# Conditioning vectors moved off the tensor engine: scale 2 and shift 2 to VectorE, three quarters of gate 1 to GpSimd

## The chip, the cores and the metric

The kernel runs on one core of one Trainium2 chip. The engines are TensorE (PE; PEld is its weight load), VectorE (DVE), ScalarE (ACT), GpSimd (POOL) and SyncE (SP), which in the kernel before issues all loads. The metric is the device time of one execution in microseconds. The times are medians of runs; the profile is of one execution.

## The reference

One layer of a hybrid decoder on x of 256 tokens by 2048. A conditioning vector c gives six vectors of 2048: shift, scale and gate for the mixers (`sh1`, `sc1`, `g1`) and for the channel mixer (`sh2`, `sc2`, `g2`).

```python
mod = (cond @ w_mod[l] + b_mod[l]).reshape(B, 6, D)      # cond = silu(c)
sh1, sc1, g1, sh2, sc2, g2 = [mod[:, i, None, :] for i in range(6)]
h = rmsnorm(x, norm_mix[l]) * (1.0 + sc1) + sh1
proj = f32(h @ w_in[l])
...                                                      # GLA, gated DeltaNet, pooling, forgetting attention
y = jnp.concatenate([y_a, y_b, y_c, y_d], axis=-1) @ w_out[l]
x = x + g1 * y
h = rmsnorm(x, norm_ffn[l]) * (1.0 + sc2) + sh2
x = x + g2 * conv_ffn(h, ...)
```

`w_mod` is 2048 by 12288, 8 MB for each 1024 of its columns. All is float32.

## The kernel before

The work goes in stages. First, shift 1 and scale 1 are summed on DVE in four groups of 512, and the input projection follows group by group (`gdn`, `extras`). From about 240 us on come the four mixers, with what is left of the input projection between them (`ex`), in the order `ORDER = "gpfd"`; then the output projection in five chunks of columns (`project`; the first into `ext`, the others into `wot`), and from about 543 us the channel mixer, whose matmuls write `fpt`. Large matmuls take each weight in two halves: `load_split` loads `wr`, ACT rounds it to `wh`, DVE subtracts to get `wl`.

The vectors wanted later are computed in the background of the mixers. A job is 1024 columns of scale 2 (`s0`, `s1`), shift 2 (`h0`, `h1`) or gate 1 (`g0`, `g1`), 16 blocks of 128 rows each. `gemv` does one job: it loads a block `wm` (128x1024, 512 KB) and multiplies it by `cond`. It has two ways:

- on PE: `cond` is broadcast to 32 columns as the weight, and four matmuls of 128x512 write four strips of 32 rows in one PSUM tile `bgt`; ACT copies the tile to `wr`, and matmuls with `sel` add the strips;
- on DVE: `accumulate` adds `wm * cond` to the tile `ga`, one instruction for each block. A matmul with `ones` then adds the 128 rows.

`to_col` puts the result along the partitions (scale, shift), `to_row` copies it to all rows (gate 1, read by the output projection as `g1t`). Which job goes where is said by two lists, and `paced` lets each list go on by its rate with every step of `ex`. A scheduler then orders all instructions, engine by engine; each engine and each queue runs its own in that order.

```python
ON_PE, PE_RATE = "s0 s1 h0", 0.38
ON_DVE, DVE_RATE = "h1 g0 g1", 0.69
```

POOL has the small powers (`rqk`, `ls`, `oss`: reciprocal square roots for the mixers), fills of zeros, and twelve compares `mk` near the start.

Of the kernel before, what the change touches and what calls it, by code (L numbers as in the profile page):

```python
# [8 lines left out]
F32 = mybir.dt.float32  # L9
# [40 lines left out]

ORDER = "gpfd"

ON_PE, PE_RATE = "s0 s1 h0", 0.38
ON_DVE, DVE_RATE = "h1 g0 g1", 0.69


def _consts():
# [16 lines left out]
def trunk_kernel(ctx: ExitStack, tc: tile.TileContext, x, c, w_mod, b_mod, norm_mix, norm_ffn, w_in,  # L74
# [18 lines left out]
    def kt_(shape, name, dt=F32):  # L93
        return keep.tile(shape, dt, name=name, tag=name)

    def mm(o, l, r, start=True, stop=True):
        PE.matmul(o, lhsT=l, rhs=r, start=start, stop=stop, skip_group_check=True)  # L97

    def tt(o, a, b, op):
        V.tensor_tensor(out=o, in0=a, in1=b, op=op)  # L100
# [28 lines left out]
    sel = kt_([P, 2], "sel")  # L129
    V.memset(sel, 0.0)  # L130
    for o in (0, 32, 64, 96):
        V.memset(sel[o:o + 1, o // 32 % 2:o // 32 % 2 + 1], 1.0)

    V1 = kt_([P, P], "V1")
    V2 = kt_([P, 54], "V2")
# [27 lines left out]
        return wh, wl  # L163


    last_wm = [None]

    def accumulate(ga, src, k, first=True):
        if k == 0 and first:
            tsc(ga, src, cond[:, k:k + 1], None, ALU.mult)  # L170
        else:
            stt(ga, src, cond[:, k:k + 1], ga, ALU.mult, ALU.add)

    def gemv(col0, done, pst=None, ready=lambda: True, bias=None):


        acc = pst() if pst else keep.tile([P, 1024], F32, name="ga", tag="ga")
        if bias is not None:
            G.memset(acc, 0.0)
            nc.sync.dma_start(acc[0:1], bias)  # L180
        for k in range(0, KT, 2):
            wms = []
            for kk in range(2):
                wms.append(wp.tile([P, 1024], F32, name="wm", tag="wm", bufs=4))
                last_wm[0] = nc.sync.dma_start(wms[kk], wm_v[:, k + kk, col0:col0 + 1024])
            for kk in range(2):
                wm = wms[kk]
                if not pst:
                    accumulate(acc, wm, k + kk, bias is None)
                    continue  # L190
                for c in range(2):
                    o = 64 * kk + 32 * c
                    mm(acc[o:o + 32], cond[:, k + kk:k + kk + 1].to_broadcast([P, 32]), wm[:, c * 512:c * 512 + 512],
                       start=k == 0, stop=k == KT - 2)
            if k == KT - 2:
                while not ready():
                    yield
                with tc.high_priority():
                    if pst:
                        gr = wp.tile([P, 1024], F32, name="wr", tag="wr", bufs=5)[:, 0:512]  # L200
                        S_.copy(gr, acc)
                        done([(gr, sel[:, c:c + 1]) for c in range(2)])
                    else:
                        done([(acc[:, c * 512:c * 512 + 512], ones) for c in range(2)])
# [23 lines left out]
    with ExitStack() as ph:  # L228
# [59 lines left out]
        with ExitStack() as st:  # L288
# [184 lines left out]
                    yield from pair(p, done[p], g + 1)  # L473
                    done[p] = g + 1

            def jobs(seq, pst):
                col = pst or (ext)
                for job in seq.split():
                    kind, n = job[0], int(job[1])
                    k0, col0 = 8 * n, dict(s=4, h=3, g=2)[kind] * D + n * 1024  # L480
                    if kind == "s":
                        yield from gemv(col0, to_col(s2, 4, k0, nffn, col), pst)
                    elif kind == "h":
                        yield from gemv(col0, to_col(sh2, 3, k0, None, col), pst)
                    else:
                        yield from gemv(col0, g1_row(n, bgt), None,
                                        lambda: "gf"[n] in emitted and "s" in emitted, b_mod[:, col0:col0 + 1024])

            emitted = set()

            def marked(steps):
                yield from steps
                emitted.add("s")


            g1t = [None, None]

            def g1_row(n, row):
                def f(parts):
                    name = ("gv", "fv")[n]  # L500
                    g1t[n] = cp.tile([P, 1024], F32, name=name, tag=name)
                    to_row(g1t[n], 0, row)(parts)
# [41 lines left out]


        bgp = ph.enter_context(tc.tile_pool(name="bgp", bufs=1, space=PSUM))
        mx = ph.enter_context(ExitStack())
        gdp = mx.enter_context(tc.tile_pool(name="gdp", bufs=2, space=PSUM, reuse_waits="tile"))
        oxp = mx.enter_context(tc.tile_pool(name="oxp", bufs=3, space=PSUM, reuse_waits="tile"))
# [190 lines left out]
        def gla(lp):  # L740
# [66 lines left out]
            for cc in range(NC - 1):  # L807
                t, os_ = cc // 2, slice((cc % 2) * CH, (cc % 2) * CH + CH)
                b = oxt().rearrange("p (f n) -> p f n", n=256)
                for f in range(2):  # L810
                    mm(b[:, f], kE2[os_, t, f * P:f * P + P], v[os_, t, f * 256:f * 256 + 256])
                s = lt([P, 2, 256], "Sg", bufs=3)
                G.memset(s, 0.0)
# [10 lines left out]
            onl = [lt(W4, f"onl{t}", tag="E", bufs=2) for t in range(NT)]  # L824
            for t in range(NT):
                b = oxt()
                for h in range(4):
                    mm(b[:, h * P:h * P + P], at[h % 2][:, t, h // 2], v[:, t, h * P:h * P + P], start=h == 0)
                for cc in (2 * t, 2 * t + 1):
                    if cc == 0:  # L830
                        continue
                    os_ = slice((cc % 2) * CH, (cc % 2) * CH + CH)
                    for f in range(2):
                        mm(b[os_, f * 256:f * 256 + 256], qT[:, f, cc * CH:cc * CH + CH], Sg[cc][:, f], start=False)
                for h in range(4):
                    jk = lt([P, P], "jl", tag="qE")
                    act(jk, b[:, h * P:h * P + P], AF.Square, accum_out=ls[:, t, h:h + 1])
                tsc(ls[:, t], ls[:, t], 1.0 / P, EPS, ALU.mult, ALU.add)
                G.tensor_tensor(out=ls[:, t], in0=ls[:, t], in1=mhalf[:, 0:4], op=ALU.pow)
                for h in range(4):  # L840
                    act(onl[t][:, h], b[:, h * P:h * P + P], AF.Copy, scale=ls[:, t, h:h + 1])
            act(flat(pr[:, 4:8]), flat(pr[:, 4:8]), AF.Silu)
# [60 lines left out]

        ex = extras(NG - 1)

        rate, owed = (PE_RATE, DVE_RATE), [0.0, 0.0]

        def paced(steps):
            for _ in steps:
# [220 lines left out]
```

## Time and profile before

| | us |
|---|---|
| median of 3 runs | 1309.63 |
| lowest and highest | 1309.63, 1311.2 |
| the profiled execution | 1305.91 |
| its span, first to last instruction | 1304.1 |

In the profile's rows a line such as L97 can be that of a helper (`mm` is L97, `tt` L100, `stt` L103), so tiles tell more than lines. A row of instructions has the engine, the operation, out<-in, the count, and times; with three numbers and slashes they are the shortest, the median and the longest in ns. A row of a stretch has its bounds, its length, then for each engine the busy time and the number of instructions.

### The profile page before, as it was taken

How to read it: one execution, taken by the hardware profiler on the slowest of the kernel's cores; microseconds unless marked ns; L12 is line 12 of the kernel's file. 1: busy time of each engine (PE TensorE's matmuls, PEld its weight loads, DVE VectorE, ACT ScalarE, POOL GpSimd, SP SyncE). 2: the span in 40 equal slices, each digit the busy share in tenths (PEclk: the TensorE clock that was granted, in tenths of full speed). 3: DMA queues.
4: the chain of work that ended last, by engine and by line, in shares of the span. 5: the costliest groups of instructions: out<-in, count | busy, mean ns of one | idle time of the engine just before them, and what ended most of it. 6: DMA issues, size and time to landing. Idle time of an engine off the chain costs nothing.

```text
span 1304.1 us, 20373 instructions
## 1 busy us (share of the span) xinstructions
PE 1251.1 (96%) x7927; PEld 1094.0 (84%) x7927; DVE 893.8 (69%) x1201; ACT 638.1 (49%) x1000; POOL 23.5 (2%) x31
## 2 busy tenths in 40 slices
PE   2799999999999999999999999999999999999996
PEld 1799999898876788888888888888888888888896
DVE  7679797989763397676656565765666597974543
ACT  3455344774354444565545554555555454443432
POOL 0200000010000100000000000000000000000000
PEclk8799999999999999999999999999999999999998
DMA  8999998796567997466666666666666699875652
GB/s 324 287 367 376 321 335 295 257 335 216 163 236 242 325 331 262 146 183 189 186 187 191 182 176 197 191 184 188 190 184 181 193 372 366 316 249 193 193 180 81
DMA packets 174231, 311.94 MB, mean 239 GB/s; under 512 B 16172, under 2 KB 65331, under 8 KB 173495
## 3 DMA queue, kind: packets, MB, share of 16 engines
q1 hardware_dynamic: 174135, 310.65, 73.3%
q8 instruction: 62, 1.02, 0.3%
q14 instruction: 34, 0.28, 0.1%
HBM read 308.51 MB, written 2.10 MB: 238 GB/s over the span
## 4 chain that ended last, share of the span: by engine, by line
PE 92%; DMA 5%; DVE 1%; ACT 1%; issue 1%; SPq 1%; POOLq 0%; ACTq 0%; DVEq 0%
PE fpt L97 57%; PE ext L97 16%; PE wot L97 5%; PE acc L97 4%; PE gdt L97 4%; DMA wm<-in_w_mod_dram 4%; PE bgt L97 3%; PE oxt L97 2%; DVE ga L103 1%; DMA wr<-in_w_in_dram 1%; DMA wsm<-in_w_in_dram 0%; ACT xT L1011 0%; DVE wl L100 0%; ACT wh L115 0%; PE oxt L873 0%
## 5 line engine op out<-in xcount | busy, mean ns | idle before, releaser
L100 DVE TENSOR_TENSOR wl<-wr,wh 128x1024 fp32r<-128x1024 f32 x384 | 468.4, 1223 | 294.2 <-ACT wh L115 293.2
L115 ACT CAST wh<-wr 128x1024 fp32r<-128x1024 f32 x384 | 402.5, 1051 | 491.4 <-PE fpt L97 306.6
L97 PE MATMUL fpt<-bigA,wh 128*128 128x512 f32 x1408 | 485.7, 397 | 2.1 <-DVE bigA L103 2.1
L97 PE MATMUL fpt<-bigA,wl 128*128 128x256 f32 x1408 | 376.2, 281 | 0.0
L97 PEld LDWEIGHTS fpt<-bigA,wh 128*128 128x128 f32 x1408 | 261.1, 188 | 62.5 <-issue 2.2
L97 PEld LDWEIGHTS fpt<-bigA,wl 128*128 128x128 f32 x1408 | 259.7, 188 | 4.8
L103 DVE SCALAR_TENSOR_TENSOR ga<-wm,cond,ga 128x1024 f32<-128x1024 f32 x139 | 177.8, 1279 | 11.3 <-DMA wm<-in_w_mod_dram 10.3
L97 PE MATMUL fpt<-wl,AH 128*128 128x512 f32 (+1 forms) x440 | 152.9, 348 | 0.0
L97 PE MATMUL fpt<-wh,AL 128*128 128x512 f32 (+1 forms) x440 | 152.5, 347 | 0.0
L97 PE MATMUL fpt<-wh,AH 128*128 128x512 f32 (+1 forms) x440 | 142.6, 348 | 0.0
L97 PE MATMUL ext<-bigA,wh 128*128 128x256 f32 x768 | 137.1, 280 | 0.0
L97 PEld LDWEIGHTS ext<-bigA,wh 128*128 128x128 f32 x768 | 117.3, 189 | 3.1 <-DVE dS L100 0.8
L97 PE MATMUL ext<-bigA,wl 128*128 128x256 f32 x384 | 107.4, 280 | 1.7 <-DVE wl L100 1.7
L97 PEld LDWEIGHTS fpt<-wh,AH 128*128 128x128 f32 x440 | 83.3, 189 | 10.8 <-ACT wh L115 0.2
L97 PEld LDWEIGHTS fpt<-wh,AL 128*128 128x128 f32 x440 | 83.3, 189 | 10.6 <-issue 0.2
L97 PEld LDWEIGHTS fpt<-wl,AH 128*128 128x128 f32 x440 | 83.3, 189 | 10.5 <-issue 0.2
L97 PEld LDWEIGHTS ext<-bigA,wl 128*128 128x128 f32 x384 | 72.1, 188 | 3.0 <-DVE wl L100 1.9
L97 PE MATMUL acc<-bigA,wh 128*128 128x256 f32 x384 | 69.0, 286 | 3.5 <-ACT bigA L115 2.8
L97 PE MATMUL ext<-wh,bigA 128*128 128x256 f32 (+1 forms) x320 | 69.5, 309 | 0.0
L97 PE MATMUL wot<-wh,bigA 128*128 128x512 f32 (+1 forms) x256 | 63.0, 337 | 0.0
L97 PEld LDWEIGHTS acc<-bigA,wh 128*128 128x128 f32 x384 | 59.6, 195 | 3.9 <-ACT bigA L115 2.9
L97 PEld LDWEIGHTS ext<-wh,bigA 128*128 128x128 f32 x320 | 53.0, 193 | 5.5 <-ACT wh L115 1.7
(340 smaller groups left out, 1187.4 us busy)
## 6 DMA issues: line engine op xcount, KB each, us to landing
wm<-in_w_mod_dram SPq DMA_DIRECT2D x192, 512.0 KB, 6.3
wr<-in_w_in_dram SPq DMA_DIRECT2D x88, 512.0 KB, 9.1
wr<-in_ffn_w_gate_dram SPq DMA_DIRECT2D x88, 512.0 KB, 4.0
wr<-in_ffn_w_up_dram SPq DMA_DIRECT2D x88, 512.0 KB, 3.9
wr<-in_ffn_w_down_dram SPq DMA_DIRECT2D x88, 512.0 KB, 4.4
wr<-in_w_out_dram SPq DMA_DIRECT2D x32, 512.0 KB, 4.4
xt<-in_x_dram SPq DMA_DIRECT2D x2, 1024.0 KB, 7.1
bigC<-in_x_dram SPq DMA_DIRECT2D x2, 1024.0 KB, 10.5
```

The source lines that it names most:

```text
L97: PE.matmul(o, lhsT=l, rhs=r, start=start, stop=stop, skip_group_check=True)
L100: V.tensor_tensor(out=o, in0=a, in1=b, op=op)
L103: V.scalar_tensor_tensor(out=o, in0=a, scalar=s, in1=b, op0=op0, op1=op1)
L115: S_.copy(hi, src)
```

## The change

- The way over PE is gone. `s0`, `s1`, `h0` and `h1` are summed on DVE.
- Gate 1 is cut into four jobs of 512 columns. `g0`, `g1`, `g2` are done by a new `gemv_pool` on POOL: for each of 16 blocks POOL issues the load of `pm` (128x512), multiplies it by `cond` in place and adds it to `gp`. There are two `pm` and three `gp`. `g3` is done on DVE, with two blocks of 512 columns in one `wm`.
- `wm` has three buffers instead of four; the GLA states `Sg` share buffers with `dd` and `E`, and `onl` is made later.
- DVE's list goes on during the output projection, with its own rate.

```diff
-ON_PE, PE_RATE = "s0 s1 h0", 0.38
-ON_DVE, DVE_RATE = "h1 g0 g1", 0.69
+ON_POOL, POOL_RATE, LAG = "g0 g1 g2", 2.2, 6
+ON_DVE, DVE_RATE, DVE_RATE_OUT = "s0 s1 h0 g3 h1", 1.4, 0.6
...
-    def gemv(col0, done, pst=None, ready=lambda: True, bias=None):
+    def gemv(col0, done, bias=None, n=1024, ready=lambda: True):
-        acc = pst() if pst else keep.tile([P, 1024], F32, name="ga", tag="ga")
+        acc = keep.tile([P, n], F32, name="ga", tag="ga", padded_shape=[P, 1024])
...
-                wms.append(wp.tile([P, 1024], F32, name="wm", tag="wm", bufs=4))
-                last_wm[0] = nc.sync.dma_start(wms[kk], wm_v[:, k + kk, col0:col0 + 1024])
-            for kk in range(2):
-                wm = wms[kk]
-                if not pst:
-                    accumulate(acc, wm, k + kk, bias is None)
-                    continue
-                for c in range(2):
-                    o = 64 * kk + 32 * c
-                    mm(acc[o:o + 32], cond[:, k + kk:k + kk + 1].to_broadcast([P, 32]), wm[:, c * 512:c * 512 + 512],
-                       start=k == 0, stop=k == KT - 2)
+            for kk in range(0, 2, nk):
+                wm = wp.tile([P, 1024], F32, name="wm", tag="wm", bufs=3).rearrange("p (k n) -> p k n", n=n)
+                last_wm[0] = nc.sync.dma_start(wm, wm_v[:, k + kk:k + kk + nk, col0:col0 + n])
+                wms += [wm[:, i] for i in range(nk)]
+            for kk in range(2):
+                accumulate(acc, wms[kk], k + kk, bias is None)
...
+            def gemv_pool(col0, done, bias, n, ready):
+                acc = bp[0].tile([P, 512], F32, name="gp", tag="gp", bufs=3)
+                G.memset(acc, 0.0)
+                G.dma_start(acc[0:1], bias)
+                for k in range(KT):
+                    pm = bp[0].tile([P, 512], F32, name="pm", tag="pm", bufs=2)
+                    G.dma_start(pm, wm_v[:, k, col0:col0 + 512])
+                    G.tensor_tensor(out=pm, in0=pm, in1=cond[:, k:k + 1].to_broadcast([P, 512]), op=ALU.mult)
+                    G.tensor_tensor(out=acc, in0=acc, in1=pm, op=ALU.add)
+                    yield
+                for _ in range(LAG):
+                    yield
+                while not ready():
+                    yield
+                with tc.issue_after(last_mm[0].ins):
+                    done([(acc, ones)])
...
-            bg = [marked(jobs(ON_PE, bgt)), jobs(ON_DVE, None)]
+            bg = [jobs(ON_POOL), jobs(ON_DVE)]
...
-                s = lt([P, 2, 256], "Sg", bufs=3)
+                s = lt([P, 2, 256], "Sg", tag="dd" if cc < 2 else "E", bufs=2)
...
-            for b_ in bg:
-                for _ in b_:
-                    pass
+            for _ in bg[0]:
+                pass
...
                 wh, wl = load_split(wo_v, ks[0], nk, c0, w)
+                owed[1] += DVE_RATE_OUT
+                while owed[1] >= 1:
+                    owed[1] -= 1
+                    next(bg[1], None)
```

What the scheduler makes of it, at two places. On PE, near the end of the mixers before the change (`gdt` is DeltaNet, `oxt` the attention, `bgt<-wm` a gate, scale or shift block):

```order
L97 MATMUL bgt_4700<-wm_4751,cond_77 32x512 x2
L97 MATMUL gdt_3111<-dS_2740,bigC_2607 64x128 x2
L873 MATMUL oxt_4518<-ident_61,p_4535 128x128 x2
L97 MATMUL bgt_4700<-wm_4757,cond_77 32x512 x2
L97 MATMUL gdt_3117<-bigC_2607,kti_2741 128x128 x4
L97 MATMUL oxt_4545<-pt_4543,fv_94 128x256
L97 MATMUL oxt_4545<-pt_4543,fv_94 128x128
L97 MATMUL oxt_4554<-pr_92 128x128
L97 MATMUL oxt_4554<-ct_85,la_4549 128x128
L97 MATMUL oxt_4554<-ngr_91,idr_90 128x128
L97 MATMUL bgt_4700<-wm_4759,cond_77 32x512 x2
L97 MATMUL gdt_3126<-X_2743,bigC_2607 64x128 x4
```

After the change no such rows are there. In their place stand four row copies of gate 1, the last of them among the first matmuls of the second projection chunk (`wot_5091` and `wot_5092`; `wh_5095` and `wh_5119` are its first two loads):

```order
L97 MATMUL wot_5092<-wh_5119,bigA_4860 128x512
L97 MATMUL wot_5091<-wh_5119,bigA_4860 128x512
L97 MATMUL wot_5091<-wl_5120,bigA_4860 128x512
L97 MATMUL wot_5091<-wh_5119,bigA_4860 128x512
L97 MATMUL wot_5092<-wh_5119,bigA_4860 128x512
L97 MATMUL wot_5092<-wl_5120,bigA_4860 128x512
L97 MATMUL bgt_4857<-gp_4790,ones_65 128x512
L97 MATMUL wot_5092<-wh_5119,bigA_4860 128x512
L97 MATMUL wot_5091<-wh_5137,bigA_4860 128x512
```

The copy waits for `gp_4790`, the third sum on POOL, and all that stands behind it on PE waits with it. In the kernel before, all of PE's blocks were done ahead of the projection, and the last copies were of sums on DVE.

On POOL before the change, from the fills to the mixers' last power:

```order
L813 MEMSET Sg_3984 128x512
L813 MEMSET Sg_3993 128x512
L813 MEMSET Sg_4002 128x512
L577 TENSOR_TENSOR rqk_2688<-rqk_2688,mhalf_78 128x16
L179 MEMSET ga_3719 128x1024
L839 TENSOR_TENSOR ls_4008<-ls_4008,mhalf_78 128x4 x2
L726 TENSOR_TENSOR oss_3132<-oss_3132,mhalf_78 128x4 x2
L179 MEMSET ga_4784 128x1024
```

The queue holds nothing else in this stretch, and its powers and fills follow each other. After the change, around the same power `rqk` (the first two steps' sums, then the loads of the next two):

```order
L468 TENSOR_TENSOR pm_3221<-pm_3221,cond_71 128x512
L468 TENSOR_TENSOR pm_3225<-pm_3225,cond_71 128x512
L469 TENSOR_TENSOR gp_3218<-gp_3218,pm_3221 128x512
L469 TENSOR_TENSOR gp_3218<-gp_3218,pm_3225 128x512
L467 DMA pm_3266<-in_w_mod_dram 128x512
L467 DMA pm_3270<-in_w_mod_dram 128x512
L579 TENSOR_TENSOR rqk_2685<-rqk_2685,mhalf_72 128x16
L468 TENSOR_TENSOR pm_3266<-pm_3266,cond_71 128x512
L468 TENSOR_TENSOR pm_3270<-pm_3270,cond_71 128x512
L469 TENSOR_TENSOR gp_3218<-gp_3218,pm_3266 128x512
```

The power stands behind two steps and ahead of the other 46. From the fifth step on a load, a product and an addition follow each other one by one:

```order
L467 DMA pm_3414<-in_w_mod_dram 128x512
L469 TENSOR_TENSOR gp_3218<-gp_3218,pm_3410 128x512
L467 DMA pm_3454<-in_w_mod_dram 128x512
L468 TENSOR_TENSOR pm_3414<-pm_3414,cond_71 128x512
L469 TENSOR_TENSOR gp_3218<-gp_3218,pm_3414 128x512
L468 TENSOR_TENSOR pm_3454<-pm_3454,cond_71 128x512
L467 DMA pm_3458<-in_w_mod_dram 128x512
L469 TENSOR_TENSOR gp_3218<-gp_3218,pm_3454 128x512
L467 DMA pm_3517<-in_w_mod_dram 128x512
L468 TENSOR_TENSOR pm_3458<-pm_3458,cond_71 128x512
L469 TENSOR_TENSOR gp_3218<-gp_3218,pm_3458 128x512
```

The load of a step is issued behind the addition two steps before it, which frees its buffer. The two powers `oss`, which DeltaNet waits for, stand behind some 40 of the 48 steps.

More of the change, by code (lines that the diff above doesn't have):

```diff
@@ L96, in mm @@
     def mm(o, l, r, start=True, stop=True):
-        PE.matmul(o, lhsT=l, rhs=r, start=start, stop=stop, skip_group_check=True)
+        last_mm[0] = PE.matmul(o, lhsT=l, rhs=r, start=start, stop=stop, skip_group_check=True)
     def tt(o, a, b, op):
@@ L127, in trunk_kernel @@
     V.memset(ones, 1.0)
[L129 to L132, printed above, removed]
     V1 = kt_([P, P], "V1")
@@ L198, in gemv @@
                 with tc.high_priority():
[L199 to L204, printed above, removed]
+                    done([(acc[:, c:c + 512], ones) for c in range(0, n, 512)])
             yield
@@ L478, in jobs @@
+            def jobs(seq):
                 for job in seq.split():
                     kind, n = job[0], int(job[1])
-                    k0, col0 = 8 * n, dict(s=4, h=3, g=2)[kind] * D + n * 1024
+                    k0 = 8 * n
                     if kind == "s":
-                        yield from gemv(col0, to_col(s2, 4, k0, nffn, col), pst)
+                        yield from gemv(4 * D + n * 1024, to_col(s2, 4, k0, nffn, bgt))
                     elif kind == "h":
-                        yield from gemv(col0, to_col(sh2, 3, k0, None, col), pst)
+                        yield from gemv(3 * D + n * 1024, to_col(sh2, 3, k0, None, bgt))
@@ L485, in jobs @@
                     else:
-                        yield from gemv(col0, g1_row(n, bgt), None,
-                                        lambda: "gf"[n] in emitted and "s" in emitted, b_mod[:, col0:col0 + 1024])
+                        c0 = 2 * D + n * 512
+                        how = (gemv_pool if n < 3 else gemv)
+                        yield from how(c0, g1_row(n // 2, n % 2 * 512, bgt), b_mod[:, c0:c0 + 512], n=512,
+                                       ready=lambda: "gf"[n // 2] in emitted)
@@ L489, in trunk_kernel, with g1_row @@
             emitted = set()
-            def marked(steps):
-                yield from steps
-                emitted.add("s")
             g1t = [None, None]
-            def g1_row(n, row):
+            def g1_row(n, c, row):
                 def f(parts):
-                    name = ("gv", "fv")[n]
-                    g1t[n] = cp.tile([P, 1024], F32, name=name, tag=name)
-                    to_row(g1t[n], 0, row)(parts)
+                    if g1t[n] is None:
+                        name = ("gv", "fv")[n]
+                        g1t[n] = cp.tile([P, 1024], F32, name=name, tag=name)
+                    to_row(g1t[n], c, row)(parts)
@@ L546, in trunk_kernel @@
         bgp = ph.enter_context(tc.tile_pool(name="bgp", bufs=1, space=PSUM))
+        bp[0] = ph.enter_context(tc.tile_pool(name="bp", bufs=1, reuse_waits="tile"))
         mx = ph.enter_context(ExitStack())
@@ L823, in gla @@
             ls = lt([P, NT, 4], "ls")
-            onl = [lt(W4, f"onl{t}", tag="E", bufs=2) for t in range(NT)]
+            onl = []
             for t in range(NT):
@@ L839, in gla @@
                 G.tensor_tensor(out=ls[:, t], in0=ls[:, t], in1=mhalf[:, 0:4], op=ALU.pow)
+                onl.append(lt(W4, f"onl{t}", tag="E", bufs=2))
                 for h in range(4):
```

7 lines of the change are left out of this document (3 added, 4 removed).

## Prediction

> **What bounds the kernel now.** I read the page's busy times and its chain first, then the busy times by stretch, then the rows of the tiles that the change moves, and last the rows of the two engines that get the work.
>
> ```profile
> span 1304.1 us, 20373 instructions
> PE 1251.1 (96%) x7927; PEld 1094.0 (84%) x7927; DVE 893.8 (69%) x1201; ACT 638.1 (49%) x1000; POOL 23.5 (2%) x31
> PE 92%; DMA 5%; DVE 1%; ACT 1%; issue 1%; SPq 1%; POOLq 0%; ACTq 0%; DVEq 0%
> 240.00:265.00 25.00, 23.72 (x189) 19.76 (x188) 24.53 (x45) 16.20 (x31) 0.00 (x0) 1.00 0.78 264
> 265.00:442.00 177.00, 176.85 (x1351) 140.92 (x1349) 116.90 (x210) 87.57 (x195) 6.74 (x4) 1.00 0.72 242
> 442.00:541.00 99.00, 99.00 (x547) 84.56 (x547) 72.88 (x83) 49.81 (x88) 4.71 (x4) 1.00 0.82 287
> ```
>
> TensorE (PE) carries 92% of the chain that ended last. The change lies between 240 and 541 us (the mixers and the output projection). In the last three rows the columns behind the length are the busy time of PE, its weight loads, VectorE (DVE), ScalarE and GpSimd (POOL), then granted clock, DMA share and GB/s. PE is full there at clock 1.00; DVE has 60 of 177 us free from 265 to 442, POOL nearly all. So a matmul taken out of this stretch is worth its time, as long as nothing else comes to end last.
>
> **What leaves the tensor engine.**
>
> ```profile
> L97 PE MATMUL bgt<-wm,cond x192: 592/592/617, 245.5 to 437.9; 128*32 128x512 f32 x192
> 240.00:541.00 301.00, 47.65 (x248) 1.00 0.76 259
> 406.60 1.95 PE L97 MATMUL bgt<-sel,wr 128*128 128x1 f32 x16
> 445.00:541.00 96.00, 4.08 (x8) 1.00 0.82 287
> ```
>
> The first row is the work itself. The second is PE's busy time on the tile `bgt` alone: 47.65 us, with four narrow matmuls lying side by side. In it are three additions of the four strips (`bgt<-sel,wr`, third row, 3 x 1.95) and the four row copies of gate 1 (last row, 4.08). So the products take 47.65 - 5.85 - 4.08 = 37.7 us. The additions shrink from 16 records to 8, which saves 3 x 1 us. Sum: 40.6 us off PE. The ends are 0 (if PE then only waits) and 43.6 (47.65 less the row copies); I take 40.6, since PE shows no gap in these stretches. The three ScalarE copies of the strips go too; ScalarE is half idle, so I count nothing.
>
> **What DVE gets.**
>
> ```profile
> 284.00:478.00 194.00, 128.59 (x232) 1.00 0.73 251
> 284.00:478.00 194.00, 30.70 (x24) 1.00 0.73 251
> 284.00:478.00 194.00, 27.01 (x23) 1.00 0.73 251
> L103 DVE SCALAR_TENSOR_TENSOR ga<-wm,cond,ga x139: 1268/1279/1286, 12.7 to 1152.4; 128x1024 f32<-128x1024 f32 x139
> L100 DVE TENSOR_TENSOR pr<-ext,pr 128x512 f32<-128x512 f32 x24 | 16.4, 685 | 7.1 <-PE ext L97 7.0
> ```
>
> The first three rows are DVE alone from 284 to 478 us (why these ends, below): in all, on the gate and scale sums `ga`, and on the weight halves `wl`. By the order after the change, DVE has 39 sums of 1024 columns and 16 of 512 in the same stretch of work: 39 x 1.279 + 16 x 0.685 (nearest row of 512 columns) = 61 us for 30.7. So its work there is 128.6 + 30 = 159 us. That alone is more than the 194 - 40 = 154 us which the shortened stretch would have.
>
> **What POOL gets: the term that decides.** Each of 48 steps is a load of 128x512 that POOL issues, a product and an addition. POOL has no such row, so I bound them.
>
> ```profile
> L813 POOL MEMSET Sg<- 128x512 f32 x3 | 1.5, 527 | 171.8 <-DVE bigA L100 171.8
> L179 POOL MEMSET ga<- 128x1024 f32 x4 | 3.8, 952 | 632.0 <-PE fpt L97 558.9 <-PE bgt L97 61.3 <-PE ext L97 11.8
> L393 POOL TENSOR_SCALAR mk<-ct x12: 523/527/1587, 43.8 to 51.2; 128x128 uint8<-128x128 f32 x12
> L185 SPq DMA_DIRECT2D wm<-in_w_mod_dram x128: 327/340/1432, 188.7 to 1142.8; - x128
> DMA to landing us min/median/max: 3.5/6.3/9.9
> ```
>
> Below, a product costs at least the write of 512 columns, 0.53 us; above, four times the compare of 128 columns, 4 x 0.527 = 2.1 us. It reads two operands of 512, so the nearest row is the one that moves 1024 columns, 0.95 us. With 0.2 us for waiting on the instruction before it I take 1.15. The Trainium skill's "GPSIMD Engine Reference" (Elementwise — side-by-side cycle accounting) gives 4497 ns for an addition of 2048 columns; a quarter of that is an estimate of 1.1 us, so by it the sum would hardly move. Issuing a load costs 0.33 to 1.43 us, the ends of SP's row for the same tensor; no POOL row is nearer, so I take the middle, 0.9. Undisturbed, a step is 2 x 1.15 + 0.9 = 3.2 us.
>
> It will be disturbed:
>
> ```profile
> 43.72 1.28 DVE L103 SCALAR_TENSOR_TENSOR ga<-wm,cond,ga 128x1024 f32<-128x1024 f32 x1
> 43.81 1.59 POOL L393 TENSOR_SCALAR mk<-ct 128x128 uint8<-128x128 f32 x1 [31.19 <-DMA ct<-in_cst_dram]
> 443.66 1.01 POOL L726 TENSOR_TENSOR oss<-oss,mhalf 128x4 f32<-128x4 f32 x1 [71.44 <-DMA wr<-in_w_out_dram]
> 451.72 1.22 DVE L100 TENSOR_TENSOR wl<-wr,wh 128x1024 fp32r<-128x1024 f32 x1
> 451.96 1.85 POOL L726 TENSOR_TENSOR oss<-oss,mhalf 128x4 f32<-128x4 f32 x1 [7.29 <-DVE oss L109]
> 279.80 1.21 DVE L100 TENSOR_TENSOR wl<-wr,wh 128x1024 fp32r<-128x1024 f32 x1
> 280.04 3.77 POOL L577 TENSOR_TENSOR rqk<-rqk,mhalf 128x16 f32<-128x16 f32 x1 [55.09 <-ACT ag L112]
> 281.15 1.28 DVE L103 SCALAR_TENSOR_TENSOR ga<-wm,cond,ga 128x1024 f32<-128x1024 f32 x1
> ```
>
> Twelve equal compares take 0.53 us each, but the first takes 1.59: it began while DVE was in a sum until 45.00. Two equal powers take 1.01 and 1.85: the second began while DVE was in a `wl` until 452.94. Each time the extra, 1.06 and 0.84 us, is what was left of the DVE instruction, less a tenth. So a POOL instruction that reads waits for the end of a DVE instruction with two SBUF inputs, and the sums and `wl` are all such. Of DVE's 159 us, 61 + 27 + some 20 (smaller ones) = 108 are of this kind, about half of the stretch. A product that comes at random then waits 0.5 x 0.6 = 0.3 us; in strict turns it waits a whole 1.2. I take 0.65, in the lower part, since half of DVE's time doesn't block. A step is 3.2 + 2 x 0.65 = 4.5 us; the ends are 3.2 and 5.6.
>
> The last two rows speak against the page that would make it worst. The Trainium skill's "SBUF — State Buffer" (Who interferes with whom) says that the two engines share a read port, and that whichever starts first holds it for its whole instruction. The power from 280.04 ran to 283.81, yet DVE's sum at 281.15 passed in its usual 1.28 us. That fits if POOL lets go once its 16 columns are read. With 512 columns the read is most of the instruction, and no run here shows that case.
>
> **When PE needs it.** The third POOL sum is waited for by a matmul behind 23 of the 24 first matmuls of the second projection chunk.
>
> ```profile
> 473.01 36.17 PE wot L97 x158
> ```
>
> That is 473.0 + 23 x 36.17/158 = 478 us now, hence 284 to 478 above. After the change it is due at 478 - 40.6 + 1 (one row copy more lies ahead) = 438 us. POOL does only two steps before the power `rqk`, which stands ahead of the third in its queue and ends at 283.8. So 46 steps and 6 us of its other work (four small powers of 1.01, four fills) remain: 284 + 6 + 46 x 4.5 = 497 us. PE waits 497 - 438 = 59 us in all; some of it falls earlier, at the first two POOL rows and at the `oss` powers, which also queue on POOL, but that isn't added. A check without waits: DVE's 108 us and 92 products at 1.0 us of reading, one after the other, end at 484.
>
> **The sum.** 59 - 40.6 = +18 us: about 1322 for the span and 1324 for the profiled time. The profiled execution took 1305.91 us, 3.7 less than the median of 1309.63, so against the median it is 1328.
>
> At nothing I count: `wm` with three buffers instead of four (a sum that is late holds its load, and behind that SP's queue of `wr` loads and so `wl`; the cover is PE's own wait; without it each case costs up to the 2.1 us that a sum waits for `wm` at most now); the same in the last stage, where gate 2 is summed beside 96% PE work; `Sg` and `onl` in shared buffers.
>
> ```profile
> DVE ga L103 <- DMA wm<-in_w_mod_dram: 10.3, 13, 2.1
> ```
>
> **Rivals.**
>
> 1. *Faster: POOL is hardly held.* Then a step is 3.2 to 4.0 us. At 3.4 POOL ends at 446, PE waits 8 us, and DVE's 159 us from 284, 95% packed, end at 451: 13 us of wait against 40.6, so -27 and 1282. It decides from 4.1 us a step on ((438 + 40.6 - 290)/46). For it: DVE stands idle for 65 of 194 us now. Against: the two waits of 1.06 and 0.84 us.
> 2. *Strict turns.* Each POOL instruction waits for a whole DVE one: 5.6 us a step, end at 548, +69, 1379. The skill's rule of the held port would give this, because DVE would always have one waiting. Against: the sum at 281.15.
> 3. *The loads end last.* With two buffers a step can't be shorter than half of issue, landing, two products and two waits: (0.9 + 6.3 + 2.3 + 1.3)/2 = 5.4 us, end at 538, +59, 1369. For it: 6.3 us median to landing. Against: these loads are 256 KB, not 512; at 4.2 us landing it gives 4.35 and hides.
> 4. *No change.* A step of 4.05 to 4.15 us.
>
> **How the numbers follow.** Forecast (4.2 to 5.2 us a step, 1314 to 1360): 0.40. Rival 1: 0.34. Rival 2: 0.08. Rival 3: 0.12. Rival 4: 0.06. About 0.2%, 2.6 us, is what a measurement of this kernel can tell from no change. So slower 0.60, same 0.06, faster 0.34. The range runs from just below rival 1's time, 1280, to 1365, which leaves out the upper rivals and the ends of the forecast, about 0.2; the forecast's own range is 1314 to 1360.
>
> **What the next profile shows.** Right: `bgt<-wm,cond` is gone; POOL is about full from 284 us, with products of over 1.15 us where DVE runs a sum or a `wl`, and adjacent products of one sum 4 to 5 us apart; PE idles for tens of us at `bgt<-gp`, waiting for POOL; `fpt` begins near 565 instead of 543 us, and from there on nothing differs. Wrong: products at 0.5 to 1.0 us, or no wait beside DVE (rival 1); PE waiting on `wl` instead of `gp`, which would make DVE the bound; POOL idle before each product until a load (rival 3).

## The result, and the profile after

| | before | after |
|---|---|---|
| median of the runs, us | 1309.63 | 1360.28 |
| lowest and highest, us | 1306.98, 1311.2 | 1358.42, 1364.99 |
| the profiled execution, us | 1305.91 | 1360.08 |

The changed kernel is slower: ratio 1.0398, with a 95% interval from 1.0376 to 1.0419. That is +51 us, where +18 was forecast (1328).

Of the changed kernel's page the span, the busy times, and the engines' shares of the chain that ended last:

```profile
span 1358.3 us, 20138 instructions
PE 1247.2 (92%) x7735; PEld 1108.5 (82%) x7735; DVE 980.6 (72%) x1228; ACT 638.3 (47%) x997; POOL 191.2 (14%) x180
PE 72%; DVE 12%; DMA 7%; issue 4%; ACT 2%; POOL 1%; SPq 1%; POOLq 0%; ACTq 0%; DVEq 0%
```

TensorE's share of the chain fell from 92 to 72%, and VectorE's rose from 1 to 12%. GpSimd, which the prediction made the end, has 1%. The stretches of the mixers and of the output projection in the changed kernel (columns as in the prediction: PE, PEld, DVE, ACT, POOL, then clock, DMA share, GB/s):

```profile
300.00:350.00 50.00, 39.89 (x302) 38.14 (x301) 50.00 (x51) 17.56 (x25) 39.64 (x32) 0.90 0.72 220
350.00:400.00 50.00, 45.19 (x329) 40.24 (x328) 49.71 (x62) 21.11 (x41) 36.08 (x31) 0.93 0.81 259
400.00:450.00 50.00, 35.26 (x193) 28.35 (x193) 47.19 (x55) 18.57 (x52) 44.58 (x44) 0.83 0.56 167
450.00:500.00 50.00, 36.20 (x203) 28.78 (x202) 40.75 (x61) 20.13 (x66) 20.56 (x20) 0.81 0.78 255
500.00:550.00 50.00, 41.39 (x166) 32.49 (x165) 28.10 (x29) 17.93 (x31) 19.38 (x16) 0.81 0.42 136
```

VectorE is full from 300 to 450 us (146.9 of 150). TensorE stands still for a fifth of that time, and its granted clock, 1.00 there in the kernel before, is 0.83 to 0.93, and 0.81 from 450 to 550 us. So TensorE's busy time fell only from 1251.1 to 1247.2 us, although 40 us of its work are gone. The stretch from 240 us to the channel mixer's first large matmul, first row before, second after:

```profile
240.00:548.20 308.20, 304.10 (x2121) 249.40 (x2119) 219.15 (x349) 160.12 (x325) 12.14 (x9) 1.00 0.75 256
```
```profile
240.00:602.40 362.40, 301.09 (x1923) 265.03 (x1923) 304.08 (x393) 159.41 (x321) 181.45 (x161) 0.89 0.68 215
```

TensorE stands still for 61.3 us there instead of 4.1. By the prediction's 40.6 us of removed work 263.5 us of the 304.1 would be left; they took 301.1, which fits the mean clock (263.5/0.89 is 296). So the stretch got 57 us of standing still and 38 us of slower work, less 40.6 us of removed work: the 54 us by which it is longer.

The channel mixer's large matmuls begin later by all of the difference. First row before, second after; the numbers behind the durations are the first and the last start:

```profile
L97 PE MATMUL fpt<-bigA,wh x1408: 388/397/502, 548.2 to 1044.4; 128*128 128x512 f32 x176
```
```profile
L97 PE MATMUL fpt<-bigA,wh x1408: 388/397/475, 602.4 to 1098.5; 128*128 128x512 f32 x176
```

From the first to the last start it is 496.2 us before and 496.1 after: nothing was lost behind the projection.

Why is VectorE full? Its groups in the changed kernel from 280 to 540 us (busy us, mean ns of one, then idle time before them):

```profile
L103 DVE SCALAR_TENSOR_TENSOR ga<-wm,cond,ga 128x1024 f32<-128x1024 f32 x43 | 66.3, 1541 | 4.7 <-DMA wm<-in_w_mod_dram 4.4
L100 DVE TENSOR_TENSOR wl<-wr,wh 128x1024 fp32r<-128x1024 f32 x28 | 40.8, 1456 | 11.3 <-ACT wh L115 11.3
L103 DVE SCALAR_TENSOR_TENSOR ga<-wm,cond,ga 128x512 f32<-128x512 f32 x16 | 19.3, 1205 | 0.1
L100 DVE TENSOR_TENSOR bigA<-pr,bigA 128x256 fp32r<-128x256 f32 x16 | 15.3, 982 | 5.7 <-ACT bigA L115 5.7
L789 DVE COPY_PREDICATED at<-mk,oxt 128x256 f32<-128x256 uint8 x12 | 6.2, 531 | 0.0
L100 DVE TENSOR_TENSOR pr<-ext,pr 128x512 f32<-128x512 f32 x8 | 5.4, 675 | 0.0
```

A sum of 1024 columns takes 1.54 us instead of 1.28, a weight half 1.46 instead of 1.22, a `bigA` half 0.98 instead of 0.42. All of these read two tensors from SBUF. The last two rows, with one operand in PSUM (`oxt`, `ext`), take what they always took. The timeline of the changed kernel near 302 us shows the mechanism (start, duration, engine):

```profile
301.42 1.04 POOL L468 TENSOR_TENSOR pm<-pm,cond 128x512 f32<-128x512 f32 x1 [2.00 <-DMA pm<-in_w_mod_dram]
...
301.62 1.91 DVE L103 SCALAR_TENSOR_TENSOR ga<-wm,cond,ga 128x1024 f32<-128x1024 f32 x1
...
302.53 2.15 POOL L469 TENSOR_TENSOR gp<-gp,pm 128x512 f32<-128x512 f32 x1
...
303.46 2.31 DVE L100 TENSOR_TENSOR wl<-wr,wh 128x1024 fp32r<-128x1024 f32 x1
...
304.64 2.02 POOL L468 TENSOR_TENSOR pm<-pm,cond 128x512 f32<-128x512 f32 x1
```

GpSimd's product runs undisturbed to 302.46. The sum began at 301.62 and ends at 303.53, which is 1.1 us behind the product's end. The addition ends 1.15 us behind the sum, the weight half 1.1 us behind the addition, the next product 0.9 us behind the weight half. They take strict turns, and each stands on its engine for about the sum of two. In the whole trace 46 of the 96 products and additions are lengthened by more than 0.15 us, and each of the 46 ends its own undisturbed time, less 0.11 to 0.14 us, behind the end of a VectorE instruction. GpSimd loses 32 us by it. What TensorE waits for in the changed kernel, and what `p` (the attention's softmax) waits for in turn (total us, times, the longest):

```profile
PE oxt L877 <- ACT p L112: 16.4, 5, 7.1
PE gdt L97 <- DVE kti L100: 8.6, 2, 6.0
PE ext L97 <- DVE wl L100: 4.8, 4, 2.2
ACT p L112 <- DVE s L872: 14.7, 6, 4.8
```

From 240 to 602 us TensorE's waits are 38 us for tiles of VectorE and 20 for tiles of ScalarE. None is for `gp`.

### The profile page after: what moved, and what is told of

Its sections match the earlier page's. It is cut to its first block, busy times and chain, and to the rows that moved or that the text cites. A ratio compares the mean times of both kernels' runs of the same rounds, so it can differ in the third digit from the quotient of the medians.

```text
span 1358.3 us, 20138 instructions
## 1 busy us (share of the span) xinstructions
PE 1247.2 (92%) x7735; PEld 1108.5 (82%) x7735; DVE 980.6 (72%) x1228; ACT 638.3 (47%) x997; POOL 191.2 (14%) x180
## 4 chain that ended last, share of the span: by engine, by line
PE 72%; DVE 12%; DMA 7%; issue 4%; ACT 2%; POOL 1%; SPq 1%; POOLq 0%; ACTq 0%; DVEq 0%
PE fpt L97 55%; PE ext L97 8%; PE wot L97 5%; DVE ga L103 4%; DMA wm<-in_w_mod_dram 3%; DMA wr<-in_w_in_dram 3%; PE acc L97 2%; DVE wl L100 2%; DVE xt L103 1%; DVE bigA L100 1%; PE oxt L97 1%; POOL pm L468 1%; PE bgt L97 1%; POOL gp L469 0%; PE gdt L97 0%
## 5 line engine op out<-in xcount | busy, mean ns | idle before, releaser
L100 DVE TENSOR_TENSOR wl<-wr,wh 128x1024 fp32r<-128x1024 f32 x384 | 475.0, 1240 | 301.9 <-ACT wh L115 301.2
L103 DVE SCALAR_TENSOR_TENSOR ga<-wm,cond,ga 128x1024 f32<-128x1024 f32 (+1 forms) x168 | 225.2, 1340 | 15.4 <-DMA wm<-in_w_mod_dram 14.1
L97 PE MATMUL ext<-bigA,wh 128*128 128x256 f32 x768 | 143.6, 289 | 5.6 <-DVE pr L100 4.3
L97 PEld LDWEIGHTS ext<-bigA,wh 128*128 128x128 f32 x768 | 122.9, 198 | 6.5 <-DVE pr L100 4.7
L97 PE MATMUL ext<-bigA,wl 128*128 128x256 f32 x384 | 110.9, 289 | 5.3 <-DVE wl L100 5.3
L97 PEld LDWEIGHTS ext<-bigA,wl 128*128 128x128 f32 x384 | 75.5, 197 | 6.8 <-DVE wl L100 6.7
L97 PE MATMUL ext<-wh,bigA 128*128 128x256 f32 (+1 forms) x320 | 77.5, 331 | 1.8 <-DVE bigA L100 1.2
L469 POOL TENSOR_TENSOR gp<-gp,pm 128x512 f32<-128x512 f32 x48 | 75.9, 1581 | 2.5
L468 POOL TENSOR_TENSOR pm<-pm,cond 128x512 f32<-128x512 f32 x48 | 65.9, 1375 | 25.1 <-DMA pm<-in_w_mod_dram 24.8
```

The costliest lines, as they stand in the source:

```text
L97: last_mm[0] = PE.matmul(o, lhsT=l, rhs=r, start=start, stop=stop, skip_group_check=True)
L103: V.scalar_tensor_tensor(out=o, in0=a, scalar=s, in1=b, op0=op0, op1=op1)
L468: G.tensor_tensor(out=pm, in0=pm, in1=cond[:, k:k + 1].to_broadcast([P, 512]), op=ALU.mult)
L469: G.tensor_tensor(out=acc, in0=acc, in1=pm, op=ALU.add)
```

## The experiments

Each time below is a median beside a median of the kernel before on the same chip (1308.7, 1308.4 and 1309.3 us in three series, on three chips, so times of different series compare to about 1 us). In the first group the program is scheduled as it is, and only then marked instructions are narrowed: `CUT` maps an instruction to (columns, r), where r over 0 turns it into a fill of its 2048 bytes per partition, 512 r elements of 4/r bytes. So the order on every engine is word for word that of the kernel from which it comes.

### GpSimd's reads and time taken away

```diff
-                    G.tensor_tensor(out=pm, in0=pm, in1=cond[:, k:k + 1].to_broadcast([P, 512]), op=ALU.mult)
-                    G.tensor_tensor(out=acc, in0=acc, in1=pm, op=ALU.add)
+                    CUT[G.tensor_tensor(out=pm, in0=pm, ..., op=ALU.mult).ins.name] = (16, 0)
+                    CUT[G.tensor_tensor(out=acc, in0=acc, in1=pm, op=ALU.add).ins.name] = (16, 0)
```

> The changed kernel, instruction for instruction in the same order, but each of GpSimd's 96 products and additions works on 16 of its 512 columns (three quarters of gate 1 come out wrong); loads, waits and copies stay. It takes away what GpSimd reads and most of the time of its steps. Theory HELD (VectorE is the bound of the mixers, and some 50 us of its time there is waiting for GpSimd's reads: 43 long sums 0.26 us too long, 16 short ones 0.52, 28 weight halves 0.23, 16 bigA halves 0.56, and so on): 1360 - 50, about 1310 us, and VectorE's sums back at 1.28 us. Theory LOAD (VectorE is full from the sums moved to it, GpSimd costs it little): 1350 to 1360. Theory QUEUE (the engines wait for what stands in GpSimd's queue, powers and sums): also about 1310, but VectorE's rows stay long.

Measured: 1310.56, ratio 1.0019 [1.0002, 1.0036]. VectorE's busy time on the page is 918.9 us instead of 980.6, with the same instructions. So GpSimd's arithmetic costs 49.7 us, and LOAD is out as the main cause. What is left of the change (40 us off TensorE, the sums on VectorE, GpSimd's loads) gains nothing.

### The same time on GpSimd, without reads

Against the edit above, fills in place of the two instructions:

```diff
-... = (16, 0)
+... = (512, 4)
```

> As before this one, in the same order, but each of GpSimd's products and additions is a fill of the same 2048 bytes per partition, byte by byte, which reads nothing and should take about 1.8 us, so that a step (load issue, two fills) takes about the 4.3 us that it takes in the changed kernel. Three quarters of gate 1 come out wrong. HELD: the reads are gone, so the time is that of the run with 16 columns, about 1310 us, within 10 us. LOAD: 1350 to 1360. QUEUE: GpSimd is as late as in the changed kernel, so 1350 to 1360.

Measured: 1350.93, ratio 1.0327 [1.0306, 1.0347]. HELD missed: the reads are gone, VectorE's rows are short again, and still it is slow. Its trace says why. The fills and a VectorE group:

```profile
L468 POOL MEMSET pm<- x48: 1794/1804/1824, 275.6 to 517.1; 128x2048 uint8 x48
```
```profile
L103 DVE SCALAR_TENSOR_TENSOR ga<-wm,cond,ga 128x1024 f32<-128x1024 f32 x43 | 55.0, 1279 | 8.4 <-DMA wm<-in_w_mod_dram 8.2
```

The larger waits for GpSimd (total us, times, the longest), and the chain of the page:

```profile
DVE oss L100 <- POOL oss L728: 17.4, 2, 15.5
ACT onl L112 <- POOL ls L842: 13.1, 2, 9.2
PEld bgt L97 <- POOL gp L469: 10.2, 1, 10.2
```
```profile
PE 72%; DMA 10%; POOL 10%; DVE 4%; issue 2%; ACT 1%; SPq 1%; POOLq 0%; ACTq 0%; DVEq 0%
```

Here the powers and the last sum do wait in GpSimd's queue, 17.4 + 13.1 + 10.2 = 40.7 us, as much as the whole difference to 1310.6 (40.4), and GpSimd has 10% of the chain. In the changed kernel the same waits are

```profile
ACT onl L112 <- POOL ls L842: 2.5, 1, 2.5
DVE oss L100 <- POOL oss L728: 1.2, 1, 1.2
```

So there are two bounds near each other: GpSimd's queue at over 4 us a step, which gives about 1351 alone, and the held VectorE, which in the changed kernel makes everything so late that almost nobody is left waiting for GpSimd.

### Fills half as long

Against the edit above:

```diff
-... = (512, 4)
+... = (512, 2)
```

> The run with fills (1351) again, with fills half as long: 1024 elements of two bytes, about 0.95 us each, so that a step takes some 2.45 us, near the 2.9 that a reading step takes undisturbed (0.58 + 1.03 + 1.27). Nothing is read, so VectorE isn't held, and GpSimd's queue is short. If the whole difference between 1310.6 and 1351 was GpSimd's queue (its trace shows 17.4 us of waiting at oss, 13.1 at ls, 10.1 at the last sum): 46 x 1.7 us less, so no wait is left: 1308 to 1316, and the changed kernel's 1360, in which nearly nobody waits for GpSimd, is then VectorE being held. If fills disturb by themselves (their writes): about 1330.

Measured: 1311.80, ratio 1.0019 [1.0002, 1.0037], as forecast. GpSimd is busy 139.9 us, VectorE 919.6 us. So neither GpSimd's writes nor a queue of 2.5 us a step costs anything that shows. VectorE's rows here, in the changed kernel's own order:

```profile
L100 DVE TENSOR_TENSOR wl<-wr,wh 128x1024 fp32r<-128x1024 f32 x46 | 56.2, 1221 | 33.0 <-ACT wh L115 33.0
L103 DVE SCALAR_TENSOR_TENSOR ga<-wm,cond,ga 128x1024 f32<-128x1024 f32 x43 | 54.9, 1278 | 6.3 <-DMA wm<-in_w_mod_dram 6.1
L103 DVE SCALAR_TENSOR_TENSOR ga<-wm,cond,ga 128x512 f32<-128x512 f32 x16 | 12.0, 750 | 0.1
L100 DVE TENSOR_TENSOR bigA<-pr,bigA 128x256 fp32r<-128x256 f32 x16 | 6.3, 420 | 5.6 <-ACT bigA L115 5.6
```

The same instructions cost VectorE 980.6 - 919.6 = 61 us more when GpSimd reads.

### Half of the reads

```diff
                     G.tensor_tensor(out=pm, in0=pm, ..., op=ALU.mult)
-                    G.tensor_tensor(out=acc, in0=acc, in1=pm, op=ALU.add)
+                    CUT[G.tensor_tensor(out=acc, in0=acc, in1=pm, op=ALU.add).ins.name] = (16, 0)
```

> The changed kernel in its own order, but only GpSimd's 48 additions are cut to 16 columns; the products stay whole (three quarters of gate 1 come out wrong). A step should take 0.58 for the load's issue, 1.1 to 2 for the product and 0.23, some 2.5 to 3 us, and GpSimd holds VectorE half as often. The run with fills (1351) showed that GpSimd's queue alone is enough for +42. If the queue is the only thing that costs: 46 steps of 3 end at 290 + 138 = 428 plus waits for data, before they are due, so about 1310, like the run with both cut. If being held costs VectorE by itself, in proportion to the reads: 1310 + half of the 50 us, about 1335, with VectorE's long sums at about 1.4 us.

Measured: 1323.14, ratio 1.0121 [1.0105, 1.0137], between the two. VectorE's long sums take 1.40 us, as expected for being held. The chain of its page:

```profile
PE 76%; DVE 11%; DMA 7%; issue 3%; ACT 1%; SPq 1%; POOLq 0%; ACTq 0%; DVEq 0%
```

GpSimd isn't in it, and the waits for its powers (1.9 us at `oss`, 1.6 at `ls`) are about those of the run with short fills (1.2 and 1.3). Here VectorE's busy time is 941.3 us, 22.4 over the run with both cut, and the time is 12.6 us over it. So being held costs by itself, with the queue short: 0.56 us for each us here. In the changed kernel it is at most 49.7/61.7 = 0.8, if all of GpSimd's cost there is being held.

### VectorE's sums taken away

```diff
             stt(ga, src, cond[:, k:k + 1], ga, ALU.mult, ALU.add)
+            # of s0, s1 and h0: CUT[...] = (16, 0)
```

> The changed kernel in the same order with GpSimd untouched, but VectorE's sums of s0, s1 and h0 work on 16 of 1024 columns from the second block on (scale 2 and half of shift 2 come out wrong). It takes some 39 sums of 1.3 to 1.5 us, 50 to 58 us, off VectorE in the mixers. HELD and LOAD: VectorE is no longer full, 1360 - 50 or less: 1280 to 1310. QUEUE: GpSimd's 48 steps are still there, held now by fewer instructions; it still ends tens of us after the 438 us at which it would be due: 1330 to 1360.

Measured: 1342.82, ratio 1.0272 [1.0248, 1.0297], in QUEUE's range; HELD and LOAD missed. Taking VectorE's new load away, 54 us of busy time, brings only 17.5 us. Now GpSimd's steps are nearer to the end (the `ls` powers are waited for 8.5 us, against 2.5). But the run doesn't speak for QUEUE alone: VectorE's busy time, 926.5 us, is still 52.6 us above that of the next run, where GpSimd is cut as well (873.9). Most of its moved sums are gone, but its being held has hardly shrunk (61 to 53 us), which HELD's range had left out.

> The changed kernel in its own order, with GpSimd's products and additions and VectorE's sums of s0, s1 and h0 all cut to 16 columns (scale 2, half of shift 2 and most of gate 1 come out wrong). With GpSimd cut alone the time was 1310.6, so the 40 us off TensorE brought nothing. If VectorE's moved sums are what used them up (LOAD): 1310 less 40, at most 1270 to 1280. If the loads or the way the work is ordered set the end: 1295 to 1310.

With GpSimd cut as well (the two edits together): 1299.46, ratio 0.9941 [0.9922, 0.9960]. Against 1310.56 the moved sums cost 11 us, not 40. LOAD missed by 20 us; the other answer, that the loads or the order set the end, has the time right, but not yet a cause. Of the 40 us that left TensorE, 9 arrive even when VectorE and GpSimd have next to nothing to do for it. TensorE's largest wait there (the transposition of `p`, the softmax's result):

```profile
PE oxt L879 <- ACT p L112: 10.5, 3, 6.2
```

The kernel before has no such wait of TensorE. That its `bgt` matmuls stood in these gaps isn't shown: in the next run, where they are cut short, no such wait opens either. Where the missing us are can be read from the same stretch as above, from 240 us to the channel mixer:

```profile
240.00:539.70 299.70, 276.81 (x1924) 247.72 (x1922) 206.89 (x392) 159.69 (x321) 77.84 (x161) 0.96 0.77 258
```

TensorE stands still for 22.9 us, 18.8 more than before, and the work that is left (263.5 us) takes 276.8, 13.3 more, at a clock of 0.96. These 32 us are the part of the 40.6 that doesn't arrive.

### What TensorE's work was worth

The kernel before, in its own order:

```diff
-                    mm(acc[o:o + 32], cond[...], wm[:, c * 512:c * 512 + 512], start=k == 0, stop=k == KT - 2)
+                    i = mm(...)
+                    if k > 0:
+                        CUT[i.ins.name] = (16, 0)
```

> The kernel before in its own order, but TensorE's matmuls of the blocks of s0, s1 and h0 take 16 of 512 columns from the third block on (scale 2 and half of shift 2 come out wrong). It shows what the removed work is worth on TensorE: 14/16 of 37.7 us is 33 us. If TensorE's time is worth its length, about 1277 us; if VectorE or the loads end just behind it, 1290 to 1305.

Measured: 1293.06, ratio 0.9891 [0.9866, 0.9917]. TensorE's time on the tile `bgt` fell from 47.65 to

```profile
240.00:541.00 301.00, 21.52 (x248) 12.64 (x248) 0.50 (x3) 4.13 (x7) 0.99 0.76 263
```

that is by 26.1 us and not by 33, since a narrow matmul still takes 0.19 us. Of these 26.1 us, 15.6 arrived: 0.6 for each. TensorE's waits for the blocks, first row before, second here:

```profile
PE bgt L97 <- DMA wm<-in_w_mod_dram: 1.4, 2, 1.3
```
```profile
PE bgt L97 <- DMA wm<-in_w_mod_dram: 6.2, 9, 1.0
```

So part of the loss is that TensorE now comes to the blocks before their loads have landed, and none of its matmuls waits for `p`. The price of 0.6 is one with these loads in the way, which the changed kernel's TensorE doesn't need.

### Nothing on GpSimd

```diff
-ON_POOL, POOL_RATE, LAG = "g0 g1 g2", 2.2, 6
-ON_DVE, DVE_RATE, DVE_RATE_OUT = "s0 s1 h0 g3 h1", 1.4, 0.6
+ON_POOL, POOL_RATE, LAG = "", 2.2, 6
+ON_DVE, DVE_RATE, DVE_RATE_OUT = "s0 s1 g0 g1 h0 g2 g3 h1", 2.4, 0.8
...
-                        how = (gemv_pool if n < 3 else gemv)
+                        how = (gemv)
```

> The changed kernel with nothing on GpSimd: all of gate 1 is summed on VectorE too, 512 columns at a time, and VectorE's list goes on at a higher rate (the scheduler orders it anew; the output is whole). VectorE gets 48 more sums of 0.74 us, 36 us, and is held by nothing. HELD (the reads cost VectorE some 45 us): 1310 to 1345, faster than the changed kernel by 15 to 50. LOAD: VectorE is full already, so 1360 + up to 36: 1360 to 1395.

Measured: 1300.15, ratio 0.9946 [0.9931, 0.9961]: faster than the changed kernel by 60 us, more than either theory said, and faster than the kernel before. The order is new too, so the 60 us needn't all come from the reads. VectorE's sums of 512 columns, 48 of them the steps that GpSimd had:

```profile
L103 DVE SCALAR_TENSOR_TENSOR ga<-wm,cond,ga 128x512 f32<-128x512 f32 x64 | 47.8, 748 | 5.0 <-DMA ga<-in_b_mod_dram 3.4 <-DMA wm<-in_w_mod_dram 0.6 <-issue 0.3
```

48 x 0.748 = 36 us, less than the 61 us that it lost by standing behind GpSimd's reads: its busy time is 950.9 us, 30 below the changed kernel's, with all of GpSimd's sums on it.

The fourth `wm` buffer back (`bufs=4`), in the same version:

> The version with everything on VectorE (1300.15), with four buffers wm instead of three. If three buffers hold the sums' loads and, behind them in SyncE's queue, the weights' loads, it gains: 1290 to 1298. If not: 1300, within 3 us.

Measured: 1295.47, ratio 0.9895 [0.9876, 0.9913], the best version here, in the range of the first answer. So three buffers cost 5 us by the medians, 7 by the ratios, in a term that the prediction had counted at nothing.

Other orders and shares did worse:

```diff
-ON_DVE, DVE_RATE, DVE_RATE_OUT = "s0 s1 g0 g1 h0 g2 g3 h1", 2.4, 0.8
+ON_DVE, DVE_RATE, DVE_RATE_OUT = "s0 g0 g1 g2 g3 s1 h0 h1", 1.8, 1.2
```

> The version with everything on VectorE, with the jobs in the order s0 g0 g1 g2 g3 s1 h0 h1 and the rates 1.8 and 1.2 instead of 2.4 and 0.8, so that more sums fall into the output projection and fewer into the mixers. VectorE is full up to 400 us and has 6 to 9 us free in each 50 us from 450 on. If its load in the mixers is what costs: 1290 to 1297. If it makes the weight halves of the projection late instead: 1303 to 1312.

Measured: 1339.88, ratio 1.0228 [1.0207, 1.0249]; both answers missed. The sums were put off too far, and the copy of shift 2 ahead of the channel mixer waits for the last ones:

```profile
PE bgt L97 <- DVE ga L103: 40.7, 2, 28.7
```

These 40.7 us are as much as the whole difference to 1300: the same work, later, is worth -8 or +31.

From the kernel before, with fewer jobs left on TensorE (and VectorE's list going on into the projection, as in the changed kernel):

```diff
-ON_PE, PE_RATE = "s0 s1 h0", 0.38
-ON_DVE, DVE_RATE = "h1 g0 g1", 0.69
+ON_PE, PE_RATE = "s0 s1", 0.38
+ON_DVE, DVE_RATE, DVE_RATE_OUT = "h1 g0 g1 h0", 0.97, 0.55
...
```

> A version that might beat both: the kernel before, but only h0 goes from TensorE to VectorE, where it is summed last and on into the output projection. TensorE loses 12.6 us of products and a strip addition; VectorE gets 16 sums of 1.28, 20.5 us, where it has about 26 us free from 443 to 541. If TensorE's time is worth half of its length (33 us were worth 15.6 in the run with short blocks): 1302. If VectorE makes the weight halves late instead: 1309 to 1320.

Measured: 1311.30, ratio 1.0022 [1.0006, 1.0038]: no gain, in the range of the second answer. But TensorE waits only 1.1 us for weight halves there, so that answer's cause isn't shown. With `"s0"` on TensorE and `"s1 g0 g1 h0 h1", 1.0, 0.75` on VectorE:

> The kernel before, with only s0 left on TensorE; s1, g0, g1, h0 and h1 are summed on VectorE in blocks of 1024, the last ones into the output projection. Between the kernel before (1308.5, three jobs on TensorE), the one with two (1311.3) and the one with none (1300.15). If TensorE's time counts at 0.6 of its length and VectorE still has room: 1300 to 1304. If VectorE's sums of 1024 cost as much as they bring: 1308 to 1313.

Measured: 1326.50, ratio 1.0130 [1.0107, 1.0153], a miss. Both have their own order; which wait costs here wasn't followed further.

## Why the prediction was wrong

The sign and the range held; the size didn't. Point by point:

- **The failed step in size: "Sum: 40.6 us off PE", taken at its full worth.** With GpSimd's arithmetic taken away the change gains nothing: 1310.56 against 1308.69, +2 us where the sum has -40.6. The sum's other term, 59 us, came out at 49.7. So the miss of 32 us comes from the first term, and the error of the second hides a part of it. The work did go. But "PE shows no gap in these stretches" was read as "TensorE is the bound", and other waits end right behind it: even with VectorE's moved sums cut too, only 9 us arrive (1299.46). The other 32 us became TensorE's standing still (18.8) and slower work (13.3), and the moved sums cost the 11 us that make +2 of -9. In the old order a us off TensorE was worth 0.6 us (15.6 of 26.1).
- **VectorE's load (159 us for 154).** As a load it was about right: the moved sums cost 11 us.
- **GpSimd's step (4.5 us).** Near in size, in part by luck. The three kinds of GpSimd instruction in the changed kernel, and three rows of its timeline, the first power, the one after the idle time, and the last addition:

```profile
L467 POOL DMA_DIRECT2D pm<-in_w_mod_dram x48: 538/577/767, 269.7 to 515.3; - x48
L468 POOL TENSOR_TENSOR pm<-pm,cond x48: 1029/1196/2028, 275.6 to 518.4; 128x512 f32<-128x512 f32 x48
L469 POOL TENSOR_TENSOR gp<-gp,pm x48: 1264/1320/2400, 278.3 to 519.5; 128x512 f32<-128x512 f32 x48
```
```profile
289.60 2.94 POOL L579 TENSOR_TENSOR rqk<-rqk,mhalf 128x16 f32<-128x16 f32 x1 [7.53 <-DVE rqk L107]
...
484.73 1.08 POOL L728 TENSOR_TENSOR oss<-oss,mhalf 128x4 f32<-128x4 f32 x1 [23.73 <-issue]
...
519.47 1.28 POOL L469 TENSOR_TENSOR gp<-gp,pm 128x512 f32<-128x512 f32 x1
```

From 292.5 to 520.75, less 23.7 of standing idle at `oss` and some 6 of other work, it is 198.5/46 = 4.3 us. The issue of a load took 0.58 us and not 0.9; an addition began 0.07 us behind its product (at 302.53 behind 302.46), where 0.2 had been counted. Being held cost GpSimd 0.66 us a step (32 us in all) and not 1.3, and waiting for loads, which the sum left out, cost 0.5 (24.8 us in 20 cases). GpSimd ended at 520.75 and not at 497, since it began its 46 steps 8.5 us later and stood idle ahead of `oss`.

- **The failed step in mechanism: "PE waits 497 - 438 = 59 us in all", with being held priced on GpSimd alone.** The prediction read from two rows that a reading GpSimd instruction waits for VectorE, and charged 2 x 0.65 us a step for it. It never charged the same wait to VectorE, which had 5 us too little room already. Measured, that is 61 us on VectorE, and it comes earlier than GpSimd's end: TensorE reached the copy of the third sum at 532.5, behind the 23 matmuls of this row of the chain, and GpSimd had been done for 12 us. The wait that was priced does exist: with fills of the same length it cost 40 us. But in the changed kernel the held VectorE comes first.

```profile
527.20 5.26 PE wot L97 x23
```

So 1328 came out as a sum of two wrong terms: some 42 us too much saved on TensorE, and 59 us of waiting in place of 49.7 us of another cause. That the second is near in size, and with it the sign and the range, is in part luck. Of the signs named for being wrong VectorE as the bound is what happened, though TensorE waits for `p` and for other tiles of VectorE more than for `wl`.
- **Rival 2, strict turns (0.08).** Its mechanism was the right one, its place and price weren't: an instruction that is held waits for the whole other one, but only 46 of GpSimd's 96 were held, so a step took 4.3 and not 5.6 us. It was marked down by the sum at 281.15 that passed beside the power `rqk`; the text itself had a reading for that, that a power of 16 columns has soon read them. The Trainium skill's "SBUF — State Buffer" (Who interferes with whom) says that a VectorE instruction with two SBUF inputs contends with a GpSimd instruction that reads SBUF and not with one that only writes it. The trace agrees: 980.6 us of VectorE's time beside reads, 919.6 beside fills.
- **Rivals 1, 3 and 4.** Undisturbed, a step would have been 0.58 + 1.03 + 1.27 = 2.9 us, yet with a step of 2.5 us and nobody held (the fills half as long) the time is 1311.8 and not 1282, since TensorE's saving isn't there to be had. The loads lengthened GpSimd's steps but weren't the end, since TensorE waits for none of its sums. The step of 4.3 us is near rival 4's, yet the time isn't the old one: the step didn't decide.
- **Counted at nothing.** Three `wm` buffers cost 5 to 7 us where that was tried. Nothing was lost in the last stage, as forecast. `Sg` and `onl` in shared buffers weren't tried by themselves.

What stays open: of the 40.6 us off TensorE, 32 don't arrive even with little else to do (1299.46). They are 18.8 us of standing still, 10.5 of them at `p`, and 13.3 us of slower work; what would win them back, beyond the fourth buffer's 5 to 7 us, wasn't found. And how the changed kernel's 49.7 us split between the held VectorE and GpSimd's queue isn't settled to the us: each alone was shown to cost (12.6 us for 22 us of being held; 40 us for steps of over 4 us), and they overlap.

## What to carry to other kernels

Before work goes from one engine to another, charge the wait for a shared resource to both sides: here 48 steps on GpSimd cost VectorE 61 us, while doing them itself costs it 36. A tensor engine that is 100% busy with background work isn't 100% bound: cut that work to a few columns in the same order, see what a us of it is worth, and read which waits open in its place. When a suspected cause is taken away and the time stays, look for a second bound right behind it: keep the instructions' time and take away their reads, then halve the time.

## What the hardware showed

- VectorE and GpSimd took strict turns for whole instructions: VectorE's sums went from 1.28 to up to 2.68 us, GpSimd's products from 1.03 to 2.03. GpSimd lost 32 us by it and VectorE 61. Beside GpSimd's fills (0.95 or 1.80 us each) VectorE's sums stayed at 1.28.
- A GpSimd product of 128x512 with a broadcast operand takes 1.03 us undisturbed, an addition of two tensors 1.27, the issue of a 256 KB load 0.58 (0.54 to 0.77).
- TensorE's granted clock was 0.81 in stretches where it was 72 to 83% busy, and 1.00 where it was full. So gaps cost more than their length here: with 57 us more of standing still, the work that was left took 38 us longer.
